# Two-layer attention trunk: layer B's first query block takes both key parts in one product, layer A's rotary key is turned before it is split, and a tenth warming product

## The chip, the core and the metric

The kernel runs on one core of a Trainium2 chip. The metric is device time in microseconds (us) from the first to the last instruction of one execution. The engines are TensorE (PE, with its weight loads shown apart as PEld), VectorE (DVE), ScalarE (ACT), GpSimd (POOL) and SyncE (SP), which issues most of the DMAs.

## What is computed

A decoder trunk of two layers over 512 tokens of width 1024, all in fp32. Layer A has multi-head latent attention (8 heads, a compressed key/value of rank 256, and one rotary key of 64 features that all heads share). Layer B has sliding-window attention: 16 query heads of 64 features over 4 shared key/value heads, in blocks of 128 queries, each of which sees its own block of keys and the one before; block 0 sees only its own. Each layer ends with a squared-ReLU MLP of width 4096, and every sum is normalised.

```python
# layer A: the scores' rotary part; k_r is one key for all heads
k_r = _rope(h[..., MLA_Q_RANK + MLA_KV_RANK:], pos)
s = (jnp.einsum('bqhc,bkc->bhqk', ql, c_kv)
     + jnp.einsum('bqhr,bkr->bhqk', qr, k_r)) * scale
...
# layer B
s = jnp.einsum('bnqkgd,bnjkd->bnkgqj', q, k_band) * SWA_HEAD_DIM ** -0.5
s = jnp.where(mask[None, :, None, None], s + bias, -jnp.inf)
m = jnp.maximum(s.max(-1), sink)
p = jnp.exp(s - m[..., None])
denom = p.sum(-1) + jnp.exp(sink - m)
o = jnp.einsum('bnkgqj,bnjkd->bnqkgd', p / denom[..., None], v_band)
```

## The kernel before, in words

**Numbers in two parts.** TensorE multiplies in a rounded fp32 form (F32R). To keep fp32 accuracy each operand is split: a high part, the rounded copy, written by ScalarE, and a low part, source minus high, written by VectorE (`split`, L75 to L83, where L77 is the copy and L80 the subtraction). A product of two such operands is three products into one bank (high by high, high by low, low by high). `group` (L102 to L106) issues the products of a bank; nearly all of TensorE's rows carry its line, L104. `pe` keeps an instruction at its place in program order on its engine; everything else may be moved by a scheduler when the program is built, which writes one fixed order for each engine. At run time each engine works through its own order, and waits on semaphores where an operand or a buffer is not ready.

**Start.** TensorE first multiplies a tile of zeros, WARM times, 512 columns each, into a bank that nobody reads (L342 to L345), while the first inputs come in. The first real products are layer A's compressed key/value: `kvb`, 320 columns for each block of 128 tokens, of which the last 64 are the rotary key.

**Layer A's rotary key** (`rot_key`, L944 to L951). For each block of tokens VectorE rotates the 64 features, writes them twice side by side, rounded, as the high part, and subtracts to get the low part; both go to `kr2`. Later, after the third block of the query latent, TensorE turns the high parts of the four blocks into one bank and the low parts into another (8 transposes, L1020), and ScalarE copies each bank to its half of `krr` (L1021). `krr` is read by layer A's scores (`scores`, L1106), from the first head on. For query block 0 layer A already takes the high and the low part of the keys in one product, 256 columns, and lets VectorE add the halves (L1125).

**Layer B's attention** (L1285 to L1383) runs over 16 heads with `run_steps`: at step u it issues the scores of head u + 2, then filling work (query products of later heads, at the end parts of the output projection), then the transposes of head u's probabilities (`turn`), then the product with the values of head u - 1 (`mix`).
- `scores`: for each of four query blocks, two products, with the keys' high part `khh` and low part `kll` (queries carry their low half in the other 64 rows). Blocks 1 to 3 have 256 keys; block 0 has 128. The four blocks fill two banks. VectorE adds the bias and takes the row maximum in one instruction for each block (L1320), then `nb` (L1324); ScalarE takes the exponentials to `p` (L1328) and that of the sink (L1332); VectorE adds and inverts the sums (L1333, L1334); GpSimd scales `p` (L1335, L1337). `p` has three buffers.
- `turn`: seven transposes (L1348, L1350), four into one "tr" bank and three into another; there are two such banks in the kernel. Each bank is emptied by a `split`: ScalarE writes `pth`, VectorE `ptl` (512 columns for the first bank, 384 for the second). The first bank's split is held behind the latest exponentials.
- `mix`: eight products; ScalarE copies the lower half of the rows (L1379), VectorE adds the halves (L1380).

After this the output projection, normalisations and the MLPs follow, the same for both layers; the change does not touch them.

Of the kernel before, what the change touches and what calls it, by code (L numbers as in the profile page):

```python
# [8 lines left out]
F32 = mybir.dt.float32  # L9
F32R = mybir.dt.float32r  # L10
AF = mybir.ActivationFunctionType
ALU = mybir.AluOpType
# [3 lines left out]
P = 128  # L16
D = 1024
S = 512
NT = S // P
# [6 lines left out]
SQH, SKVH, SHD = 16, 4, 64  # L26
# [5 lines left out]
LN_EPS, RMS_EPS = 1e-5, 1e-6  # L32
BANDW = 384
POOL_O, POOL_SO = (0, 2), (0, 1, 2)
WARM = 9

ON_POOL = ("w_h", "w_o", "w_sq", "w_so")

# [10 lines left out]
def build(tc, nc, io, out):  # L49
    with ExitStack() as top:  # L50
# [11 lines left out]
        def nm(s):  # L62
            n_names[0] += 1
            return f"{s}_{n_names[0]}"

        def bank(cols=512, tag="mm", bufs=6):
            return ps.tile([P, cols], F32, tag=tag, bufs=bufs, name=nm(tag), padded_shape=[P, 512])

        def tbank():
            return bank(512, "tr", 2)  # L70

        def f32(ap):
            return ap.bitcast(F32)

        def split(dst_h, dst_l, src, engine=None, keep=False):  # L75

            high = nc.scalar.activation(dst_h, src, AF.Copy)  # L77
            if keep:
                pe(high)
            low = (engine or nc.vector).tensor_sub(dst_l, src, f32(dst_h))  # L80
            if pinned[0] and engine is None:
                pe(low)
            return high, low  # L83

        def pe(ins):
            tc.keep_in_program_order(ins)
# [15 lines left out]
        def group(dst, pairs, first=True, last=True, **kw):  # L102
            for i, (st, mv) in enumerate(pairs):
                pe(nc.tensor.matmul(  # L104
                    dst, st, mv, start=first and i == 0, stop=last and i == len(pairs) - 1, **kw
                ))  # L106
# [237 lines left out]
        b = bank()  # L344
        group(b.rearrange("p (a b) -> p a b", a=4), [(zeros, zeros[:, None, :].broadcast_to([P, 4, P]))] * WARM)  # L345
        dummy = cp.tile([P, 1], F32, name="dummy")
# [32 lines left out]
        ident = cp.tile([P, P], F32, name="ident")  # L379
# [502 lines left out]
        with tc.tile_pool(name="mla", bufs=1) as mp:  # L882
# [11 lines left out]
            khh, kll = krr[:, 0, :], krr[:, 1, :]  # L894
# [34 lines left out]
            def rope(dst, src, t, n, other):  # L929

                s = src.rearrange("p (h d) -> p h d", h=n)
                d = dst.rearrange("p (h d) -> p h d", h=n)
                w = other.rearrange("p (h d) -> p h d", h=n)
                cb = cos[:, t : t + 1, :].broadcast_to([P, n, 64])
                nc.vector.tensor_mul(d, s, cb)
                for a, b in ((0, 32), (32, 0)):
                    sb = sin[:, t : t + 1, a : a + 32].broadcast_to([P, n, 32])
                    nc.vector.tensor_mul(w[:, :, a : a + 32], s[:, :, b : b + 32], sb)
                nc.vector.tensor_add(dst, dst, other)


            kr2 = mp.tile([P, 2, NT, P], F32, tag="kk", bufs=2, name=nm("kr2"))

            def rot_key(t, b):  # L944
                kr = sp.tile([P, 2, 64], F32, tag="kr", bufs=2, name=nm("kr"))
                rope(kr[:, 0, :], b[:, 256:320], t, 1, kr[:, 1, :])
                dup = kr[:, 0:1, :].broadcast_to([P, 2, 64])
                hh = kr2[:, 0, t, :].rearrange("p (a b) -> p a b", a=2)
                ll = kr2[:, 1, t, :].rearrange("p (a b) -> p a b", a=2)
                nc.vector.tensor_copy(hh.bitcast(F32R), dup)  # L950
                nc.vector.tensor_sub(ll, dup, hh)  # L951


            kvb = [bank(320) for _ in range(NT)]
# [30 lines left out]
            for t in range(NT):  # L985
                with tc.high_priority():
                    kvn.append(normed(kvb[t], KVR))
                rot_key(t, kvb[t])
# [6 lines left out]
            def query_latent(t, ks):  # L995
                tk = slice(t * P, (t + 1) * P)
                for k in ks:
                    wh, wl = ws[k // 2]
                    c = slice(k % 2 * QR, (k % 2 + 1) * QR)
                    group(qb[t], three(x0.h(k, tk), x0.l(k, tk), wh[:, c], wl[:, c]), k == 0, k == 7)  # L1000

            for t in range(NT):
                if t != 1:
                    qb[t] = bank(QR)
                if t == 0:
                    qb[1] = bank(QR)
                    for tt in range(2):
                        query_latent(tt, range(6))
                query_latent(t, range(6 if t < 2 else 0, KD))
                if t == 0:  # L1010
                    bias_bands()
                if t == 1:
                    with tc.high_priority():
                        normed_t(kvn, range(2), gkv, ckv)
                if t == 2:
                    with tc.high_priority():
                        for part, dst in ((0, khh), (1, kll)):
                            pt = tbank()
                            for tt in range(NT):
                                pe(nc.tensor.transpose(pt[:, tt * P : (tt + 1) * P], kr2[:, part, tt, :], ident))  # L1020
                            nc.scalar.activation(dst, pt, AF.Copy)  # L1021
                with tc.high_priority():
                    qn.append(normed(qb[t], QR))

# [173 lines left out]
            for t in range(2):  # L1198
                for kp in range(3):
# [3 lines left out]
            state["hold"] = hold  # L1203
            head_queries(1)
            run_steps([(h, i) for h in range(H) for i in range(NT)], AHEAD_S, scores, turn, mix, fill, NT, 2,
                      [lambda kp=kp: proj.part(2, kp) for kp in range(2)])

# [10 lines left out]
        mlp_pool[0] = None  # L1218

        with tc.tile_pool(name="swa", bufs=1) as mp:  # L1220
            khh = [mp.tile([P, S], F32R, name=nm("skh")) for _ in range(SKVH)]
            kll = [mp.tile([P, S], F32R, name=nm("skl")) for _ in range(SKVH)]

            def keys(m, cols, b):

# [41 lines left out]
            bias = [None] * 8  # L1267
# [29 lines left out]
            def scores(h, _):  # L1297
                j = h // GRP
                q = qs[h]
                nb = sp.tile([P, NT], F32, tag="nb", bufs=3, name=nm("nb"))  # L1300
                sm = sp.tile([P, NT], F32, tag="sm", bufs=3, name=nm("sm"))
                ri = sp.tile([P, NT], F32, tag="ri", bufs=3, name=nm("ri"))
                bs = []
                for n2 in range(2):
                    b = bank().rearrange("p (a b) -> p a b", a=2)
                    bs.append(b)
                    for a in range(2):
                        n = 2 * n2 + a
                        lo_c = P if n == 0 else 0
                        kc = slice(0, P) if n == 0 else slice((n - 1) * P, (n + 1) * P)  # L1310
                        tq = slice(n * P, (n + 1) * P)
                        group(b[:, a, lo_c:], [(q[:, tq], khh[j][:, kc]), (q[:, tq], kll[j][:, kc])])

                mx = bs[0][:, 0, 0:NT]
                for n2 in range(2):
                    for a in range(2):
                        n = 2 * n2 + a
                        lo_c = P if n == 0 else 0
                        b = bs[n2]
                        nc.vector.tensor_tensor_reduce(  # L1320
                            out=b[:, a, lo_c:], in0=b[:, a, lo_c:], in1=bias[h // 2][:, h % 2, lo_c:], op0=ALU.add,
                            op1=ALU.max, scale=1.0, scalar=NEG, accum_out=mx[:, n : n + 1],
                        )
                nc.vector.tensor_scalar(nb, mx, sink8[:, h : h + 1], -SWA_SCALE, ALU.max, ALU.mult)  # L1324
                p = mp.tile([P, NT, 256], F32, tag="p", bufs=3, name=nm("p"))
                for n in range(NT):
                    lo_c = P if n == 0 else 0
                    state["exp"] = nc.scalar.activation(  # L1328
                        p[:, n, lo_c:], bs[n // 2][:, n % 2, lo_c:], AF.Exp, bias=nb[:, n : n + 1],
                        scale=SWA_SCALE, accum_out=sm[:, n : n + 1],  # L1330
                    )
                nc.scalar.activation(ri, nb, AF.Exp, bias=sink[:, h : h + 1])  # L1332
                nc.vector.tensor_add(sm, sm, ri)  # L1333
                nc.vector.reciprocal(ri, sm)  # L1334
                nc.gpsimd.tensor_mul(p[:, 0, P:], p[:, 0, P:], ri[:, 0:1].broadcast_to([P, P]))  # L1335
                rest = ri[:, 1:].unsqueeze(2).broadcast_to([P, NT - 1, 256])
                nc.gpsimd.tensor_mul(p[:, 1:, :], p[:, 1:, :], rest)  # L1337
                ps_of[h] = p
# [180 lines left out]
```

## Time and profile before

| | us |
|---|---|
| median of 3 runs (range) | 997.25 (997.22 to 997.62) |
| span of the profiled execution | 997.4 |
| TensorE busy | 986.3 (99%) |
| VectorE busy | 771.9 (77%) |
| ScalarE busy | 554.7 (56%) |
| GpSimd busy | 216.5 (22%) |
| layer B's attention, 539 to 625: span, TensorE busy | 86.0, 84.27 |

How to read it: busy times are sums over the whole span, and the engines work side by side. A row of the timeline is start, duration, engine, line, operation, the tiles (written <- read), the shape and the count, and in brackets the idle time before it with what ended it. TensorE's products are pipelined and their ends modelled, so two neighbours' rows overlap; what one of them costs is read from start to start. Rows of groups give count, busy time and mean duration in ns. A wait's row gives the total, the number of times and the longest.

### The profile page before, as it was taken

How to read it: one execution, taken by the hardware profiler on the slowest of the kernel's cores; microseconds unless marked ns; L12 is line 12 of the kernel's file. 1: busy time of each engine (PE TensorE's matmuls, PEld its weight loads, DVE VectorE, ACT ScalarE, POOL GpSimd, SP SyncE). 2: the span in 40 equal slices, each digit the busy share in tenths (PEclk: the TensorE clock that was granted, in tenths of full speed). 3: DMA queues.
4: the chain of work that ended last, by engine and by line, in shares of the span. 5: the costliest groups of instructions: out<-in, count | busy, mean ns of one | idle time of the engine just before them, and what ended most of it. 6: DMA issues, size and time to landing. Idle time of an engine off the chain costs nothing.

```text
span 997.4 us, 15835 instructions
## 1 busy us (share of the span) xinstructions
PE 986.3 (99%) x6107; PEld 890.0 (89%) x6107; DVE 771.9 (77%) x1243; ACT 554.7 (56%) x850; POOL 216.5 (22%) x203
## 2 busy tenths in 40 slices
PE   9999999999999999999999999999999999999997
PEld 8988888998999999998898998889998999999986
DVE  5589967989778769877586778698985986898756
ACT  5457643467537637636145888546763664664620
POOL 0231101122212211210002775212131122123000
PEclk9999999999999999999999999999999999999999
DMA  7431126389879977963232212259798798798422
GB/s 249 143 89 54 64 106 224 92 174 243 157 171 241 175 174 202 230 118 125 87 106 96 85 65 75 96 158 208 195 187 187 166 214 175 162 263 147 117 93 85
DMA packets 60679, 149.55 MB, mean 150 GB/s; under 512 B 5260, under 2 KB 10301, under 8 KB 60605
## 3 DMA queue, kind: packets, MB, share of 16 engines
q0 software_dynamic: 24320, 58.73, 32.9%
q1 hardware_dynamic: 36140, 89.56, 27.1%
q8 instruction: 48, 0.79, 0.3%
q10 hardware_dynamic: 144, 0.26, 0.1%
q14 instruction: 27, 0.21, 0.1%
HBM read 146.41 MB, written 4.22 MB: 151 GB/s over the span
## 4 chain that ended last, share of the span: by engine, by line
PE 96%; DVE 2%; ACT 1%; DMA 1%; issue 0%; POOL 0%; DVEq 0%; SPq 0%; ACTq 0%
PE mm L104 88%; PE tr L104 5%; PE tr L1159 1%; PE tr L663 1%; PE tr L1348 1%; ACT wh L77 1%; PE tr L1350 0%; DMA raw<-in_w_kv 0%; PE tr L437 0%; DMA raw<-in_w_h 0%; DVE mm L1320 0%; DVE ptl L80 0%; PE tr L924 0%; DVE ql L80 0%; POOL wl L80 0%
## 5 line engine op out<-in xcount | busy, mean ns | idle before, releaser
L104 PE MATMUL mm<-wh,fac 128*128 128x512 f32 (+1 forms) x944 | 292.8, 387 | 0.0
L77 ACT ACTIVATE wh<-wq 128x1024 fp32r<-128x1024 f32 x164 | 173.6, 1060 | 183.6 <-PE mm L104 131.4
L80 DVE TENSOR_TENSOR wl<-wq,wh 128x1024 fp32r<-128x1024 f32 x164 | 199.7, 1222 | 70.9 <-ACT wh L77 70.1
L104 PE MATMUL mm<-xth,wh 128*128 128x256 f32 (+1 forms) x928 | 243.7, 291 | 0.0
L104 PE MATMUL mm<-xth,wl 128*128 128x256 f32 (+1 forms) x800 | 233.5, 292 | 0.0
L104 PEld LDWEIGHTS mm<-wh,fac 128*128 128x128 f32 x944 | 176.3, 188 | 35.4 <-DVE fac L80 0.6
L104 PE MATMUL mm<-xtl,wh 128*128 128x256 f32 (+1 forms) x672 | 197.4, 294 | 0.0
L104 PE MATMUL mm<-wl,fac 128*128 128x512 f32 (+1 forms) x472 | 182.4, 387 | 0.0
L104 PEld LDWEIGHTS mm<-xth,wh 128*128 128x128 f32 x928 | 168.9, 192 | 3.1
L104 PEld LDWEIGHTS mm<-xth,wl 128*128 128x128 f32 x800 | 153.4, 192 | 2.6
L77 ACT ACTIVATE wh<-raw 128x1024 fp32r<-128x1024 f32 (+3 forms) x86 | 85.0, 989 | 95.1 <-PE mm L104 56.4
L199 POOL DMA_DIRECT2D wq<-in_up x64 | 77.5, 1228 | 257.7 <-DVE wl L80 189.0
L104 PEld LDWEIGHTS mm<-xtl,wh 128*128 128x128 f32 x672 | 128.9, 192 | 3.0
L80 DVE TENSOR_TENSOR wl<-raw,wh 128x1024 fp32r<-128x1024 f32 (+2 forms) x66 | 77.1, 1174 | 35.1 <-ACT wh L77 34.7
L104 PEld LDWEIGHTS mm<-wl,fac 128*128 128x128 f32 x472 | 88.9, 188 | 16.6
L199 POOL DMA_DIRECT2D wq<-in_down x48 | 42.0, 875 | 187.5 <-DVE wl L80 181.6
L80 POOL TENSOR_TENSOR wl<-raw,wh 128x1024 fp32r<-128x1024 f32 (+2 forms) x20 | 41.2, 2063 | 87.6 <-ACT wh L77 81.9
L104 PE MATMUL mm<-wh,oh 128*128 128x512 f32 x128 | 50.9, 398 | 0.0
L104 PE MATMUL mm<-wh,ol 128*128 128x512 f32 x128 | 50.2, 392 | 0.0
L104 PE MATMUL mm<-wl,oh 128*128 128x512 f32 x128 | 50.0, 390 | 0.0
L398 POOL TENSOR_TENSOR rs<-mv,half 128x1 f32<-128x1 f32 x16 | 11.0, 689 | 167.2 <-DVE mv L419 167.1
L563 DVE TENSOR_TENSOR x<-mm,x 128x512 f32<-128x512 f32 (+1 forms) x49 | 32.9, 676 | 14.5 <-PE mm L104 14.5
(217 smaller groups left out, 1822.3 us busy)
## 6 DMA issues: line engine op xcount, KB each, us to landing
wq<-in_up POOLq DMA_DIRECT2D x64, 512.0 KB, 8.5
wq<-in_down POOLq DMA_DIRECT2D x48, 512.0 KB, 7.1
wq<-in_up SPq DMA_DIRECT2D x32, 512.0 KB, 7.0
raw<-in_down SPq DMA_DIRECT2D x28, 512.0 KB, 6.8
wq<-in_down SPq DMA_DIRECT2D x24, 512.0 KB, 5.4
raw<-in_up SPq DMA_DIRECT2D x16, 512.0 KB, 4.6
raw<-in_w_o SPq DMA_DIRECT2D x8, 512.0 KB, 4.2
raw<-in_w_sq SPq DMA_DIRECT2D x8, 512.0 KB, 3.3
```

What stands on the lines that cost most here:

```text
L77: high = nc.scalar.activation(dst_h, src, AF.Copy)
L80: low = (engine or nc.vector).tensor_sub(dst_l, src, f32(dst_h))
L104: pe(nc.tensor.matmul(dst, st, mv, start=first and i == 0, stop=last and i == len(pairs) - 1, **kw))
L199: nc.gpsimd.dma_start(half(a, jp), chunk(*more, jp), accum_op=ALU.add)
L398: nc.gpsimd.tensor_tensor(r, v, half, ALU.pow)
L563: nc.vector.tensor_add(xs[t][:, c], b, xs[t][:, c])
L663: pe(nc.tensor.transpose(pt[:, a, :], xs[t][:, k * P : (k + 1) * P], ident))
L1159: pe(nc.tensor.transpose(pt[:, kb * P : (kb + 1) * P], p[:, kb * P : (kb + 1) * P], ident))
L1348: pe(nc.tensor.transpose(pt[:, a, 0:P], p[:, kb, P:256], ident))
```

## The change

Three edits. (1) In layer B the keys' two parts lie side by side in one tile `kk`, and block 0's two products of 128 columns become one of 256, over two runs of 128; VectorE adds the first half of the result to the bias into `p`, and the maximum of block 0 takes that sum in place of the bias. `p` is therefore claimed before the maxima and no longer after them. The products of the other blocks stay. (2) In layer A the rotary key is written once, in fp32, turned with four transposes into one bank, and split from there: high part by ScalarE, low part by VectorE. (3) WARM goes from 9 to 10. The scheduler's order on TensorE and SyncE differs by nothing else; on VectorE, ScalarE and GpSimd it also differs within layer B's attention.

```diff
-WARM = 9
+WARM = 10
...
-            kr2 = mp.tile([P, 2, NT, P], F32, tag="kk", bufs=2, name=nm("kr2"))
+            kr2 = mp.tile([P, NT, P], F32, tag="kk", bufs=2, name=nm("kr2"))
...
                 dup = kr[:, 0:1, :].broadcast_to([P, 2, 64])
-                hh = kr2[:, 0, t, :].rearrange("p (a b) -> p a b", a=2)
-                ll = kr2[:, 1, t, :].rearrange("p (a b) -> p a b", a=2)
-                nc.vector.tensor_copy(hh.bitcast(F32R), dup)
-                nc.vector.tensor_sub(ll, dup, hh)
+                nc.vector.tensor_copy(kr2[:, t, :].rearrange("p (a b) -> p a b", a=2), dup)
...
-                        for part, dst in ((0, khh), (1, kll)):
-                            pt = tbank()
-                            for tt in range(NT):
-                                pe(nc.tensor.transpose(pt[:, tt * P : (tt + 1) * P], kr2[:, part, tt, :], ident))
-                            nc.scalar.activation(dst, pt, AF.Copy)
+                        pt = tbank()
+                        for tt in range(NT):
+                            pe(nc.tensor.transpose(pt[:, tt * P : (tt + 1) * P], kr2[:, tt, :], ident))
+                        split(khh, kll, pt)
...
-            khh = [mp.tile([P, S], F32R, name=nm("skh")) for _ in range(SKVH)]
-            kll = [mp.tile([P, S], F32R, name=nm("skl")) for _ in range(SKVH)]
+            kk = [mp.tile([P, 2, S], F32R, name=nm("skk")) for _ in range(SKVH)]
+            khh, kll = [[k[:, part, :] for k in kk] for part in range(2)]
...
-                        group(b[:, a, lo_c:], [(q[:, tq], khh[j][:, kc]), (q[:, tq], kll[j][:, kc])])
-
+                        if n == 0:
+                            both = b[:, 0, :].rearrange("p (a b) -> p a b", a=2)
+                            group(both, [(q[:, tq], kk[j][:, :, kc])])
+                        else:
+                            group(b[:, a, :], [(q[:, tq], khh[j][:, kc]), (q[:, tq], kll[j][:, kc])])
+
+                p = mp.tile([P, NT, 256], F32, tag="p", bufs=3, name=nm("p"))
+                first = p[:, 0, 0:P]
+                nc.vector.tensor_add(first, bs[0][:, 0, 0:P], bias[h // 2][:, h % 2, P:])
...
-                            out=b[:, a, lo_c:], in0=b[:, a, lo_c:], in1=bias[h // 2][:, h % 2, lo_c:], op0=ALU.add,
+                            out=b[:, a, lo_c:], in0=b[:, a, lo_c:],
+                            in1=first if n == 0 else bias[h // 2][:, h % 2, :], op0=ALU.add,
                             op1=ALU.max, scale=1.0, scalar=NEG, accum_out=mx[:, n : n + 1],
...
-                p = mp.tile([P, NT, 256], F32, tag="p", bufs=3, name=nm("p"))
```

## The prediction, made before the changed kernel ran

> **What bounds the kernel now.** I read the page first (busy shares and the chain that ended last), then the groups of instructions by form on TensorE, then the timeline of the three places that the change touches, then the waits inside layer B's attention.
>
> ```profile
> span 997.4 us, 15835 instructions
> PE 986.3 (99%) x6107; PEld 890.0 (89%) x6107; DVE 771.9 (77%) x1243; ACT 554.7 (56%) x850; POOL 216.5 (22%) x203
> ...
> PE 96%; DVE 2%; ACT 1%; DMA 1%; issue 0%; POOL 0%; DVEq 0%; SPq 0%; ACTq 0%
> ```
>
> TensorE (PE) is busy for 99% of the span and makes 96% of the chain. So the price of a product is the time until the next one starts, and whatever it frees comes off the end, unless PE then waits elsewhere. PE waits little, and in layer B's attention only for VectorE (DVE); the stage's row follows the wait's (PE 84.27, PEld 75.71, DVE 64.59, ACT 71.53, POOL 54.01 of 86 us).
>
> ```profile
> PE tr L1348 <- DVE ptl L80: 1.7, 3, 0.9
> ```
>
> ```profile
> 539.00:625.00 86.00, 84.27 (x554) 75.71 (x553) 64.59 (x230) 71.53 (x214) 54.01 (x44) 1.00 0.24 80
> ```
>
> **Layer B: 32 short products become 16.** The timeline of one head's eight score products (head 13, the other heads look alike):
>
> ```profile
> 608.12 0.27 PE L104 MATMUL mm<-skh,q 128*128 128x128 f32 x1
> 608.23 0.27 PE L104 MATMUL mm<-skl,q 128*128 128x128 f32 x1
> 608.35 0.33 PE L104 MATMUL mm<-skh,q 128*128 128x256 f32 x1
> 608.51 0.28 PE L104 MATMUL mm<-skl,q 128*128 128x256 f32 x1
> 608.63 0.28 PE L104 MATMUL mm<-skh,q 128*128 128x256 f32 x1
> ...
> 609.11 0.40 PE L104 MATMUL mm<-wh,oh 128*128 128x512 f32 x1
> ```
>
> Eight products take 609.11 - 608.12 = 0.99 us. From start to start a 256-wide product takes 0.12 (608.51 to 608.63); the two 128-wide ones take 608.35 - 608.12 = 0.23 together, so each costs as much as a 256-wide one. Seven products should take 0.88: the first 256-wide one keeps its 0.16. That is 0.11 a head. For heads 0 to 2, whose scores follow 512-wide products, I reckon 0.09 (estimate: the first short product is partly hidden there). Sum: 13 x 0.105 + 3 x 0.09 = 1.6 us. That the moving operand is now two runs of 128 costs nothing: layer A already reads krr so, at 286 ns mean, where head 13's unbroken 256-wide products last 0.28.
>
> ```profile
> L104 PE MATMUL mm<-krr,qr 128*128 128x256 f32 x24 | 5.6, 286 | 0.0
> ```
>
> [...] Head 13's rows say 0.23 against 0.12 us; the measurement decides.
>
> Added are 16 tensor_adds on DVE. Layer A has the same one (L1125, 128x128 out of a bank), 284 ns:
>
> ```profile
> L1125 DVE TENSOR_TENSOR p<-mm,const x8: 274/284/293, 64.2 to 131.5; 128x128 f32<-128x128 f32 x8
> ```
>
> That is 16 x 0.29 = 4.6 us. DVE idles 86 - 64.6 = 21 us in the stage, so its total hides the adds. They do lengthen a chain: scores, the maxima (L1320), nb, exponentials, the copies out of the transposes' two "tr" banks (pth on ScalarE, then ptl on DVE), and the next head's transposes, which need those banks. The add waits for PE's products, which the maximum waited for already; p has three buffers, and the transposes that free the oldest precede these products on PE, so its earlier claim costs nothing. If that cover were gone, each add would cost 0.3.
>
> Where that chain is late is the end of the stage, heads 10 to 12. DVE first, then PE:
>
> ```profile
> 608.79 0.68 DVE L1292 TENSOR_TENSOR q<-mm,q 64x512 fp32r<-64x512 f32 x1
> 609.40 0.28 DVE L1320 CUSTOM_DVE_ANT_0 mm<-mm,bias 128x128 f32<-128x128 f32 x1
> ...
> 609.72 0.43 DVE L1320 CUSTOM_DVE_ANT_0 mm<-mm,bias 128x256 f32<-128x256 f32 x1
> ...
> 610.74 0.66 DVE L80 TENSOR_TENSOR ptl<-tr,pth 128x512 fp32r<-128x512 f32 x1
> ...
> 616.51 0.66 DVE L80 TENSOR_TENSOR ptl<-tr,pth 128x512 fp32r<-128x512 f32 x1
> 617.10 0.68 DVE L1380 TENSOR_TENSOR o<-mm,low 64x512 f32<-64x512 f32 x1
> ```
>
> ```profile
> 611.55 0.30 PE L1348 MATMUL tr<-ident,p 128*128 128x128 f32 x1 [0.89 <-DVE ptl L80]
> ...
> 617.23 0.33 PE L1348 MATMUL tr<-ident,p 128*128 128x128 f32 x1 [0.66 <-DVE ptl L80]
> ```
>
> These are the first and the last of the three waits, each for a ptl. DVE works in program order, and the changed program's order differs here by more than the two adds, so I rework it on before's clock. After q ends at 609.40 DVE issues ptl384 of head 10, the add and the first two maxima of head 13, sm, recip, then ptl512 of head 10. By the rows' spacings: 609.40 + 0.55 (ptl384) + 0.3 (add) + 0.32 and 0.45 (maxima) + 0.2 (sm, recip) + 0.59 (ptl512, as 616.51 to 617.10) = 611.8. Until the next ptl512 (head 11) come two maxima, q and two o (0.61 each, as 608.79 to 609.40), ptl384, the second add, head 14's four maxima and four tiny ones: 0.9 + 1.8 + 0.55 + 0.3 + 1.7 + 0.5 + 0.59 = 6.3, so it ends at 618.1. Before it ended at 617.1. Head 12's second half of transposes therefore starts about 1.0 later than at 617.23; PE needs 0.1 less from there to head 13, so the tail gives back about 0.9 us. That is the largest uncertain term. Its ends: a gain of 0.8 (half of the 1.7 of waits goes) and a loss of 2 (they more than double). I take the 0.9, since the reckoning follows DVE's known order.
>
> Earlier, at heads 3 to 10, the same bank is the tight spot. Head 7's rows, DVE first, then the start of PE's next transposes:
>
> ```profile
> 589.20 0.66 DVE L80 TENSOR_TENSOR ptl<-tr,pth 128x512 fp32r<-128x512 f32 x1
> 589.77 0.21 DVE L1324 TENSOR_SCALAR nb<-mm,sink 128x4 f32<-128x4 f32 x1
> 589.90 0.55 DVE L80 TENSOR_TENSOR ptl<-tr,pth 128x384 fp32r<-128x384 f32 x1
> ```
>
> ```profile
> 590.31 0.27 PE L1348 MATMUL tr<-ident,p 128*128 128x128 f32 x1
> ```
>
> The first bank is free at 589.77, the second at 590.45, and the transposes want them at 590.31 and, four of 0.11 later, 590.75: 0.54 and 0.30 of cover. The add takes 0.3 and PE's earlier arrival 0.1, which leaves from 0.1 to -0.1. In all I count 0.2 for these heads.
>
> Layer B: -1.6 + 0.9 + 0.2 = -0.5.
>
> **Layer A: the rotary key.** Eight transposes become four, one ScalarE copy goes, four DVE subtractions of 0.29 go, and one of a 512-wide bank comes.
>
> ```profile
> L1020 PE MATMUL tr<-ident,kr x8: 272/272/273, 35.9 to 36.7; 128*128 128x128 f32 x8
> L951 DVE TENSOR_TENSOR kr<-kr,kr x4: 281/292/292, 24.7 to 28.4; 128x128 f32<-128x128 f32 x4
> ```
>
> ```profile
> L104 PE MATMUL mm<-krr,qr x56: 278/337/398, 63.5 to 139.7; 128*128 128x256 f32 x24, 128*128 128x384 f32 x16, 128*128 128x512 f32 x16
> ```
>
> Starts run from 35.9 to 36.7 for eight: 0.11 apart, so 4 x 0.11 = 0.44 us off PE, which never waits there. The low half now follows the high one by a DVE pass over 512 columns (0.66, as ptl), near 38; its first reader is at 63.5, which hides it 25 us deep. Without that cover it would cost 0.7. The key is written by 28.4 and turned at 35.9, so the four subtractions were hidden and are worth nothing.
>
> **The tenth warming product.**
>
> ```profile
> 1.00 4.21 PE L104 MATMUL mm<-zeros 128*128 128x512 f32 x9 [1.00 <-POOL zeros L343]
> 5.74 1.44 PE L104 MATMUL mm<-wh,xth 128*128 128x320 f32 x4 [0.53 <-ACT wh L77]
> 8.03 1.27 PE L104 MATMUL mm<-wl,xth 128*128 128x320 f32 x4
> 9.10 0.92 PE L104 MATMUL mm<-wh,xth 128*128 128x320 f32 x4
> 9.86 0.74 PE L104 MATMUL mm<-wh,xtl 128*128 128x320 f32 x4
> 10.44 0.75 PE L104 MATMUL mm<-wl,xth 128*128 128x320 f32 x4
> ```
>
> The nine end at 5.21; the first real product then waits 0.53 for its weights. A tenth costs about 0.43 (4.21 less the first one's latency, over nine) and ends near 5.64, before 5.74: it is hidden by that wait. If the weights came 0.5 earlier it would cost its 0.43. Its worth is the other question. Four 320-wide products take 9.10 - 8.03 = 1.07 us until about 9.4 and 10.44 - 9.86 = 0.58 after: TensorE runs at nearly half rate for 3.7 us of real work, in spite of 4.2 us of warming. A gap of 0.53 lies between the two. If closing it brought the full rate forward to the first real products, the 3.7 us hold 3.7 / 0.267 = 14 of them, each 0.12 cheaper (1.07 - 0.58 over four): 1.7 us saved. The ends are 0 and 1.7; I take 0, because nine products and 4.2 us did not do it, and a gap of 0.1 remains.
>
> [...]
>
> **Sum.** Forecast: -0.44 (A) - 0.5 (B) + 0 (warming) = -0.94 on the profiled 997.4. The median of the runs is 997.25, 0.15 below; so 996.3.
>
> **Rivals.**
> 1. [...] Chance 0.38.
> 2. The tail gives nothing back, and layer B keeps its 1.6: -2.0, 995.2. For it: PE waits only 1.7 in all now. Against: DVE's order above. 0.08.
> 3. On the other side: DVE's longer chain holds up PE at every head, not only at the last. Place: ptl before the transposes, heads 3 to 10. Price: the 0.3 of the add at each of the eight heads, up to +2.4, in all +1.5, 998.7. It decides from 0.12 a head (0.94 / 8) on. For it: head 7's cover, which the add uses up. Against: DVE has 21 us idle in the stage. 0.08.
> 4. The change does not save what it says: with the short products no dearer than half a long one, B loses the 0.9 and 0.2 and gains nothing: -0.44 + 1.1 = +0.7, 997.9. Head 13's rows speak against it. 0.04.
>
> **How the numbers follow.** The forecast has 0.42; its own range is 995.3 to 997.4. A measurement of this kernel can tell about 0.2%, 2.0 us, from no change. Faster by more than that: 0.7 of rival 1 (its -2.5 lies just beyond, within about 0.9 either way), half of rival 2 and a little of the forecast, 0.33. Slower by over 2.0: the far part of rival 3, 0.04. The rest, 0.63, is within. The range for 8 in 10 reaches from rival 1 with a milder tail, 994.0, to the near part of rival 3, 998.0; about 0.1 is left out below it and 0.07 above.
>
> **What would show it.** 112 score products in place of 128, seven in 0.88 us a head; four transposes near 36; the zeros x10, and the first real product still at 5.74. [...] For the tail: a transpose of head 12 that starts about 1.0 late against head 10's, waiting for ptl, and no other long wait before it. It is wrong if PE's waits in layer B come to under 1 us or over 4, or if the 256-wide first product takes over 0.2.

## The result

The changed kernel takes **999.93 us** (median of 20 runs, 998.63 to 1001.97); the kernel before, on the same chips, 997.74 (20 runs, 996.74 to 999.91). The ratio is 1.002, 95% interval 1.0013 to 1.0026: 2.2 us slower, and outside the range of the forecast (994.0 to 998.0).

The device time of a run is its span and about 1.75 us (1.72 to 1.95 in all runs): the profiled execution after has a span of 998.1 and a time of 999.86. So the profiled execution before, span 997.4, would by that have a time of some 999.1 (an estimate, as its own time is not on record) and not 997.25: at its start TensorE took 1.06 to 1.23 us for a group of four products until about 9.4, where the profiles of e1_warm, e2_key and the changed kernel show 0.58 or 0.59 from 6.4 on at the latest (below).

The page of the changed kernel (span; busy times; the chain by engine):

```profile
span 998.1 us, 15800 instructions
...
PE 984.5 (99%) x6088; PEld 886.3 (89%) x6088; DVE 777.7 (78%) x1256; ACT 555.0 (56%) x849; POOL 216.4 (22%) x203
...
PE 91%; DVE 3%; ACT 2%; DMA 2%; issue 1%; POOL 0%; SPq 0%; DVEq 0%; ACTq 0%
```

TensorE is busy 1.8 us less, but before's slow start (about 1.7 us) is in that difference, so it is not the work saved. Its share of the chain fell from 96 to 91%: VectorE, ScalarE and DMA are longer links of it. TensorE's waits over the whole span (total, times, longest), then layer B's stage, 539 to 625:

```profile
PE tr L1351 <- DVE ptl L80: 2.8, 3, 2.0
...
PE mm L104 <- ACT p L1331: 0.7, 3, 0.4
PE tr L437 <- DVE xtl L80: 0.5, 1, 0.5
PE tr L663 <- DVE x L425: 0.5, 1, 0.5
```

```profile
539.00:625.00 86.00, 82.67 (x530) 73.23 (x529) 69.52 (x244) 70.32 (x212) 54.00 (x44) 1.00 0.22 75
```

VectorE's busy time in the stage rose from 64.59 to 69.52, the added sums, and TensorE's fell from 84.27 to 82.67: the work left it, and the time became idle time. The waits for `ptl` rose from 1.7 to 2.8; three waits for `p` are new. Where they stand, in TensorE's timeline (the bracket is the idle time before the row and what ended it):

```profile
564.43 0.50 PE L104 MATMUL mm<-xth,wh 128*128 128x512 f32 x1 [0.41 <-ACT p L1331]
...
586.15 0.50 PE L104 MATMUL mm<-xth,wh 128*128 128x512 f32 x1 [0.17 <-ACT p L1331]
...
607.88 0.50 PE L104 MATMUL mm<-wh,oh 128*128 128x512 f32 x1 [0.17 <-ACT p L1331]
...
610.58 0.33 PE L1351 MATMUL tr<-ident,p 128*128 128x128 f32 x1 [0.58 <-DVE ptl L80]
...
616.94 0.33 PE L1351 MATMUL tr<-ident,p 128*128 128x128 f32 x1 [2.00 <-DVE ptl L80]
...
618.21 1.04 PE L104 MATMUL mm<-skk,q 128*128 128x256 f32 x7
619.09 0.40 PE L104 MATMUL mm<-wh,oh 128*128 128x512 f32 x1
```

The last two rows show the saving as forecast: seven score products in 619.09 - 618.21 = 0.88 us, where eight took 0.99. But behind the scores of heads 5, 9 and 13 the filling products wait for a bank that ScalarE's exponentials, those of heads 4, 8 and 12, have not finished reading, and head 12's second half of transposes waits 2.00 us, where it waited 0.66. The start and layer A:

```profile
1.00 4.53 PE L104 MATMUL mm<-zeros 128*128 128x512 f32 x10 [1.00 <-POOL zeros L343]
5.63 0.86 PE L104 MATMUL mm<-wh,xth 128*128 128x320 f32 x4
6.33 0.75 PE L104 MATMUL mm<-wh,xtl 128*128 128x320 f32 x4
...
34.16 0.60 PE L1016 MATMUL tr<-ident,kr 128*128 128x128 f32 x4
34.52 0.42 PE L104 MATMUL mm<-wh,xth 128*128 128x384 f32 x1
```

Here groups of four already start 0.58 apart from about 6 on (6.33 to 6.91 in the next row), which is the upper end of the prediction's warming term (1.7 us), and four transposes stand in layer A in place of eight. The profile's own clock does not tell the two starts apart: from 5.74 to 9.50 it gives a granted clock of 1.00 (third figure from the end) in both kernels, where TensorE issues 14 products before and 26 after. Before's row:

```profile
5.74:9.50 3.76, 3.76 (x14) 3.76 (x15) 3.47 (x7) 2.80 (x6) 0.00 (x0) 1.00 1.03 363
```

So that the clock was what held up before's start is inferred from the rate (1.07 us in place of 0.58 for a group of four); no figure shows it.

### The profile page after: what moved, and what is told of

The parts are those of the page before. It is cut to its first block, busy times and chain, and to the rows that moved or that the text cites. A ratio compares the mean times of both kernels' runs of the same rounds, so it can differ in the third digit from the quotient of the medians.

```text
span 998.1 us, 15800 instructions
## 1 busy us (share of the span) xinstructions
PE 984.5 (99%) x6088; PEld 886.3 (89%) x6088; DVE 777.7 (78%) x1256; ACT 555.0 (56%) x849; POOL 216.4 (22%) x203
## 4 chain that ended last, share of the span: by engine, by line
PE 91%; DVE 3%; ACT 2%; DMA 2%; issue 1%; POOL 0%; SPq 0%; DVEq 0%; ACTq 0%
PE mm L104 84%; PE tr L104 5%; ACT wh L77 1%; PE tr L1155 1%; PE tr L663 1%; DMA wq<-in_up 1%; DMA raw<-in_w_v 1%; PE tr L1351 1%; ACT p L1331 1%; DMA raw<-in_w_kv 0%; DVE x L425 0%; DVE wl L80 0%; PE tr L1353 0%; DMA raw<-in_w_h 0%; DVE mm L1323 0%
```

## The experiments

**Theory 1.** The added sum lengthens the chain from the scores to the exponentials; what TensorE saves turns into waits, above all at head 12. **Theory 2**, the rival, differs from run to run: the scheduler's new order, the sum as mere VectorE time, or a chain in which TensorE's pause is a symptom only. Each kernel was timed beside the kernel before (997.2 to 997.6 each time), 11 runs of each (5 of e3_swa, e9_late and e11_late_key_free); ratios are against it. One more term came up on the way: the granted clock.

### The three edits one by one

e1_warm has only `WARM = 10`, e2_key only the edit of the rotary key, e3_swa only layer B's. e4_swa_add is e3_swa with the merged product taken apart again, so that only the sum is added:

```diff
-                            both = b[:, 0, :].rearrange("p (a b) -> p a b", a=2)
-                            group(both, [(q[:, tq], kk[j][:, :, kc])])
+                            for part in range(2):
+                                group(b[:, 0, part * P : (part + 1) * P], [(q[:, tq], kk[j][:, part, kc])])
```

> Only the tenth warming product. In the profile of the changed kernel the products ran at the full rate from the first real one (start 5.63 against 5.74, shift -1.7 us by 9.5). If the clock's rise is the gap's doing, this alone gains up to 1.7 us in a run whose clock rose late, about 1 us in the median, and nothing elsewhere: -1.0. Rival (the rise falls by chance, whatever the tenth product): 0 within 0.3.

> Only layer A's key turned in fp32. Four transposes of 0.11: -0.44 us at 36 us, and if TensorE stays the bound, at the end too. Rival (an earlier TensorE only waits for later DMAs, as the changed kernel did at 518 and 656): 0.

> Only layer B's edit. Theory 1 (the added VectorE step and the order that comes with it delay the exponentials and the tr banks): slower, +2 to +3.5 us in all, with TensorE waits of 4 to 6 us in layer B's attention. Theory 2 (layer B loses little and the rest is DMA chance outside it): -0.5 to +0.5.

> Layer B's edit with the two short products kept apart (high part to the first half of the bank, low part to the second, then the same VectorE addition): the addition without the saved product. Theory 1: 1.6 us above the kernel with the product merged, +3.5 to +5 against before. Theory 2: TensorE hides the addition, +0 to +0.5.

| | median us (range) | ratio, 95% |
|---|---|---|
| e1_warm | 997.71 (997.17 to 998.91) | 1.0005 (0.9996 to 1.0014) |
| e2_key | 997.86 (996.74 to 999.31) | 1.0005 (0.9996 to 1.0014) |
| e3_swa | 1000.78 (1000.60 to 1001.07) | 1.0035 (1.0023 to 1.0048) |
| e4_swa_add | 999.28 (997.83 to 999.57) | 1.0013 (1.0005 to 1.0022) |

Warming and key are worth nothing that can be measured; all of the loss is layer B's edit, and there the sum alone costs less than the sum with the saving, which theory 1 did not say. That the early full rate does not need the tenth product is seen in e2_key's record, which has nine and a longer gap behind them (1.02 us) than before:

```profile
1.00 3.64 PE L104 MATMUL mm<-zeros 128*128 128x512 f32 x9 [1.00 <-POOL zeros L343]
5.67 0.86 PE L104 MATMUL mm<-wh,xth 128*128 128x320 f32 x4 [1.02 <-ACT wh L77]
6.36 0.74 PE L104 MATMUL mm<-wh,xtl 128*128 128x320 f32 x4
6.94 0.75 PE L104 MATMUL mm<-wl,xth 128*128 128x320 f32 x4
```

Groups of four are 0.58 apart from the second one on, so the rise at 9.4 in the profile of before was that execution's. What made e3_swa dearer than e4_swa_add is in its windows (busy of PE, PEld, DVE, ACT, POOL; granted clock; DMA) and in its TensorE rows:

```profile
609.00:618.00 9.00, 6.37 (x43) 5.26 (x43) 7.70 (x30) 7.44 (x24) 4.56 (x5) 1.00 0.14 54
618.00:622.00 4.00, 4.00 (x18) 3.63 (x18) 2.65 (x9) 1.93 (x7) 2.22 (x3) 0.57 0.02 4
622.00:627.00 5.00, 5.00 (x31) 4.35 (x30) 1.96 (x8) 2.76 (x11) 1.29 (x1) 1.00 0.00 2
```

```profile
617.09 0.33 PE L1355 MATMUL tr<-ident,p 128*128 128x128 f32 x1 [2.02 <-DVE ptl L80]
...
618.61 1.80 PE L104 MATMUL mm<-skk,q 128*128 128x256 f32 x7
620.21 0.63 PE L104 MATMUL mm<-wh,oh 128*128 128x512 f32 x1
620.63 0.63 PE L104 MATMUL mm<-wl,oh 128*128 128x512 f32 x1
...
621.48 0.39 PE L104 MATMUL mm<-wh,oh 128*128 128x512 f32 x1
```

Head 12's pause is 2.02 us, and behind it the granted clock is 0.57 over 618 to 622: seven score products take 620.21 - 618.61 = 1.60 in place of 0.88, for about 3.4 us (618.0 to 621.4). The fall follows that pause, with another of 0.60 at 610.7 before it; in the profile of the whole change, pauses of 2.00 (616.94) and 0.58 (610.58) left the clock at 1.00.

### Is the clock part of the price? The pause filled

Six products of zeros, 1.4 us, between the halves of head 12's transposes, into the bank that the next product claims anyway; e5_fill on e3_swa (the other engines' orders stay the same), e10_after_fill on the whole change, e15_add_fill on e4_swa_add, e16_before_fill on the kernel before:

```diff
+FILL = 6
...
+                    if h == 12 and k2 == 1:
+                        early[0] = bank()
+                        group(
+                            early[0].rearrange("p (a b) -> p a b", a=4),
+                            [(zeros, zeros[:, None, :].broadcast_to([P, 4, P]))] * FILL,
+                        )
                     pt = tbank().rearrange("p (a b) -> p a b", a=2)
...
-                b = bank()
+                b = early[0] if h == 11 else bank()
```

> Layer B's edit alone, and six products of zeros (128x512, 0.23 us each, 1.4 us) put between the two halves of head 12's transposes, where TensorE stood still for 2.0 us; the orders of VectorE, ScalarE and GpSimd are those of e3_swa. Theory 1: the pause itself costs what the four engines' chain makes of it, and on top of it the granted clock falls to half for 3.4 us after it (e3_swa's record shows 0.57 over 618 to 622), 1.7 us more; with the pause filled the clock stays at 1.00 and the time falls from 1000.8 to 998.9 to 999.4. Theory 2: the chain from scores to exponentials alone sets the end, and the clock's fall is made up behind it: 1000.6 to 1001.1, unchanged.

> The whole change, with six products of zeros (1.4 us) in head 12's pause, as in e5_fill. Theory 1: the change's own time, 999.9, has executions with and without the fall of the clock after head 12 (998.6 to 1002.0); filled, those above 1000 go and the median is 998.3 to 999.0. Theory 2: the spread has another source and the fill only delays: 999.8 to 1000.5.

> e4_swa_add (two products kept apart, VectorE's sum added: 999.28, 997.8 to 999.6) with six products of zeros in head 12's pause, which was 1.4 us there. Theory 1: the pause was near what costs the clock, so its slower executions lost it; filled, 997.8 to 998.5. Rival: its 1.8 us are the chain alone and the products of zeros, as long as the pause, add nothing or a little: 999.2 to 999.7.

> The kernel before with six products of zeros (1.4 us) in head 12's pause of 1.7 us. Theory 1: most executions of the kernel before keep their clock there, so the median stays at 997.1 to 997.5, and the few above 998.5 (5 or 6 in 27) go. Rival: the clock has no part in before's spread: the same median and the same few above 998.5.

| | unfilled | filled (range) | ratio of the filled, 95% |
|---|---|---|---|
| e5_fill | 1000.78 | 998.74 (997.94 to 999.71) | 1.0016 (1.0007 to 1.0025) |
| e10_after_fill | 999.93 | 998.36 (997.36 to 998.79) | 1.0006 (0.9997 to 1.0015) |
| e15_add_fill | 999.28 | 998.62 (998.08 to 1000.54) | 1.0017 (1.0008 to 1.0025) |
| e16_before_fill | 997.43 | 997.71 (997.32 to 1000.44) | 1.0008 (0.9999 to 1.0017) |

More work made two kernels faster: by 2.0 us where the fall is on record, and by 1.6 on the whole change, of whose 20 unfilled runs 17 lie above the slowest filled one (998.79). e5_fill's record, windows and TensorE:

```profile
609.00:618.00 9.00, 7.94 (x53) 6.87 (x54) 7.02 (x27) 7.48 (x25) 5.21 (x6) 1.00 0.02 7
618.00:622.00 4.00, 4.00 (x26) 3.46 (x25) 3.47 (x13) 1.25 (x3) 2.75 (x3) 1.00 0.00 0
```

```profile
613.55 1.64 PE L105 MATMUL mm<-zeros 128*128 128x512 f32 x6
615.81 0.33 PE L1363 MATMUL tr<-ident,p 128*128 128x128 f32 x1 [0.61 <-DVE ptl L81]
...
617.09 1.05 PE L105 MATMUL mm<-skk,q 128*128 128x256 f32 x7
617.97 0.40 PE L105 MATMUL mm<-wh,oh 128*128 128x512 f32 x1
```

TensorE still waits for `ptl`, so the fill took nothing from the chain; but it is busy, and the clock stays at 1.00. For the whole change the clock is argued from this: the fill's gain is measured (the ratios fall from 1.0020 to 1.0006), but in the one record of the unfilled change the clock stays at 1.00 behind the pause, and yet its time, 999.86, is the median. That execution loses time elsewhere: TensorE waits 0.49 us at 517 and 0.47 at 656, each behind a weight transfer of 6 us, which neither e3_swa nor e10_after_fill shows there. From head 15's scores to the end it takes 379.9 us, e10_after_fill 378.8, and e3_swa, with the fall, 380.4. On the kernel before there is nothing to win, and the two late runs there (above 1000) stay. The expectations speak of a pause of 1.7 at its head 12; that is the sum of three waits (0.89, 0.18 and 0.66), of which the last alone stands where the fill goes. With the sum alone (e15_add_fill) the medians differ by 0.7 and the ratios hardly, which leaves it open whether that kernel loses its clock.

### What does the sum cost without the clock?

e6_merge keeps the merged product and leaves out the sum. The two parts change places in `kk`, so that the maximum reads the high part's scores, and the low part of the first block's keys is missing from the scores:

```diff
-            khh, kll = [[k[:, part, :] for k in kk] for part in range(2)]
+            kll, khh = [[k[:, part, :] for k in kk] for part in range(2)]
...
-                first = p[:, 0, 0:P]
-                nc.vector.tensor_add(first, bs[0][:, 0, 0:P], bias[h // 2][:, h % 2, P:])
...
-                            in1=first if n == 0 else bias[h // 2][:, h % 2, :], op0=ALU.add,
+                            in1=bias[h // 2][:, h % 2, lo_c:], op0=ALU.add,
```

> The merged product alone: the first block's low-part scores are computed in the same product but not added (VectorE's added sum is left out, so the low part of the first block's keys is missing from the scores). TensorE's saved 0.1 us a head is there, VectorE's chain is that of before. Theory 1: TensorE comes 1.6 us sooner to a bank that comes free no sooner, so the pause at head 12 grows from 1.7 to about 3 us, nothing is gained (997.0 to 997.6), and in those executions in which the clock then falls to half 1.7 us are lost (up to 999.2). Theory 2, the added sum is the whole cost and the saved products count in full: 995.8 to 996.3.

Measured: 996.44 (995.68 to 999.07), ratio 0.9995 (0.9986 to 1.0004), 0.8 below before by the medians, though the interval does not exclude no gain, and below theory 1's range: head 12's pause does not grow (0.70, before 0.66). That VectorE's and ScalarE's work starts with the scores and moves up with them would explain it. TensorE's rows of the first score products of heads 3 and 10 and of head 12's second half, first of e6_merge, then of the changed kernel:

```profile
552.54 0.36 PE L104 MATMUL mm<-skk,q 128*128 128x256 f32 x1
...
589.73 0.45 PE L104 MATMUL mm<-skk,q 128*128 128x256 f32 x2
...
614.75 0.33 PE L1353 MATMUL tr<-ident,p 128*128 128x128 f32 x1 [0.70 <-DVE ptl L80]
```

```profile
552.37 0.48 PE L104 MATMUL mm<-skk,q 128*128 128x256 f32 x2
...
590.68 0.45 PE L104 MATMUL mm<-skk,q 128*128 128x256 f32 x2
```

Head 10's in the kernel before, for comparison:

```profile
591.96 0.27 PE L104 MATMUL mm<-skh,q 128*128 128x128 f32 x1
```

Heads 3 to 10 take 37.19 us without the sum and 38.31 with it, 1.1 more; from there to head 12's second half (616.94 in the changed kernel) 25.02 and 26.26, 1.2 more. Together 2.4; and e5_fill against e6_merge, timed side by side, says 998.74 - 996.44 = 2.3.

That is the price of the sum together with the order that the scheduler made for it, and at heads 3 to 10 the order takes part. There the scores of most heads follow each other after 5.28 to 5.42 us, but from head 5 to 6 it is 5.98 and from head 9 to 10 5.73, where e6_merge takes 5.34 and 5.33. That is 0.64 and 0.40 more, nearly the whole 1.1, from recorded waits of 0.41 and 0.17. Just ahead of the exponentials that these waits end with (those of heads 4 and 8) ScalarE's order has a copy to `pth`, which takes 0.37. First the changed kernel at head 4, then e4_swa_add at head 8:

```profile
562.62 0.59 ACT L1287 ACTIVATE q<-mm 64x512 fp32r<-64x512 f32 x1
563.11 0.47 ACT L77 ACTIVATE pth<-tr 128x384 fp32r<-128x384 f32 x1
563.48 0.35 ACT L1331 ACTIVATE p<-mm,nb 128x128 f32<-128x128 f32 x1
```

```profile
585.12 0.59 ACT L1291 ACTIVATE q<-mm 64x512 fp32r<-64x512 f32 x1
585.62 0.35 ACT L1335 ACTIVATE p<-mm,nb 128x128 f32<-128x128 f32 x1
```

In the kernel before and in e6_merge the exponentials of heads 4, 8 and 12 follow `q` directly, and no such wait is there. e4_swa_add has the sum in the same place and, of these three heads, the copy ahead at head 4 alone; it waits once, 0.31 behind head 5's scores. So the sum without the copy ahead made no wait there, in a kernel whose TensorE is 0.1 a head slower; no run keeps the sum and the saved products and changes this order alone, which leaves the shares of sum and order open.

### Can the wait be taken away?

e7_free (on e3_swa) and e8_base_free (on before) let head 11's first split, whose `ptl` head 12's transposes wait for, go before the exponentials of head 13:

```diff
-                        with behind((state["exp"],)):
+                        with behind(None if h in (11,) else (state["exp"],)):
```

e12_key_free is e8_base_free with layer A's key as in the change. e17_key_so3 has the key and moves the 1.23 us split of a weight chunk, which stands ahead of head 12's maxima on VectorE, to GpSimd (`POOL_SO = (0, 1, 2, 3)`); e18_key_free_so3 has both.

> Layer B's edit alone, with head 11's first split (four transposes, 512 wide) no longer held in turn behind the exponentials of head 13. Theory 1: head 12's second half of transposes waits for this split to free its bank; released, the wait falls from 2.0 us to under 0.7, the clock stays at 1.00, and the time falls from 1000.8 to 997.3 to 998.5. Theory 2: the chain through maxima and exponentials sets the end and the split of 0.6 us on ScalarE and 0.7 on VectorE now stands ahead of it: 1000.6 to 1001.5.

> The kernel before, with head 11's first split no longer held in turn behind the exponentials of head 13; nothing else changed. Theory 1: the 1.7 us for which TensorE waits at head 12 shrink by about 1 us, and the executions that lose the clock there go: 996.0 to 996.9, against 997.4. Theory 2: no gain, or 0.3 to 0.6 later, as the split stands ahead of the exponentials: 997.4 to 998.0.

> Layer A's rotary key as in the change and head 11's first split not held, layer B's products as before. Theory 1: e8_base_free's 997.1 less up to 0.4: 996.6 to 997.1. Rival: the key's 0.4 us is taken up again by waits behind layer A, as in e2_key: 997.1 to 997.5.

> Layer A's key as in the change, layer B's products as before, and the split of the fourth output-weight chunk (1.23 us on VectorE at 607.5, ahead of head 12's maxima) moved to GpSimd (2.4 us there). Theory 1 (VectorE's chain sets the wait of 1.7 us at head 12): 0.5 to 1.2 below the kernel before, 996.1 to 996.9. Rival (GpSimd's 2.4 us stand in the way of its products with the reciprocals, or the chain through ScalarE's exponentials is as late): 997.0 to 998.0.

> e17_key_so3 with head 11's first split not held in turn behind head 13's exponentials. Theory 1: the two take the same wait away, so no more than 0.3 below the better of e12_key_free (997.0) and e17_key_so3: 996.0 to 996.8. Rival: as e12_key_free, 996.9 to 997.5.

| | median us (range) | ratio, 95% |
|---|---|---|
| e7_free | 998.01 (997.23 to 1000.64) | 1.0010 (1.0001 to 1.0019) |
| e8_base_free | 997.08 (995.97 to 998.45) | 0.9996 (0.9987 to 1.0005) |
| e12_key_free | 997.03 (996.23 to 998.17) | 0.9997 (0.9988 to 1.0005) |
| e17_key_so3 | 997.62 (996.91 to 998.23) | 0.9997 (0.9988 to 1.0006) |
| e18_key_free_so3 | 997.98 (996.88 to 999.69) | 1.0004 (0.9995 to 1.0014) |

e7_free gains 2.8 us on e3_swa, as theory 1 expected, but its waits in layer B's stage say that most of it is not the wait:

```profile
PE mm L104 <- ACT p L1335: 2.4, 4, 1.2
PE tr L1355 <- DVE ptl L80: 0.6, 1, 0.6
```

The wait for `ptl` fell from 2.6 to 0.6, and that for the exponentials rose from 0.6 to 2.4: one long pause became several shorter ones, of 3.0 us in all against 3.2, and the clock stayed at 1.00. On the kernel before, whose record shows the clock at 1.00 there, the same edit gains nothing certain. e17_key_so3 is a miss for theory 1, by the same exchange (its waits over the whole span):

```profile
PE tr L1344 <- DVE nb L1320: 0.9, 1, 0.9
...
PE mm L104 <- ACT p L1324: 0.7, 1, 0.7
```

No wait for `ptl` is left, and 1.6 us of others stand there, where before had 1.7. No version was found that is measurably faster than the kernel before and computes the same.

### Is it the sum's place or its length?

e9_late takes block 0's maximum over the high part alone and adds the low part behind the last maximum; the first block's exponential goes last. For that the four maxima needed a place of their own:

```diff
-                nc.vector.tensor_add(first, bs[0][:, 0, 0:P], bias[h // 2][:, h % 2, P:])
-                mx = bs[0][:, 0, 0:NT]
+                mx = sp.tile([P, NT], F32, tag="mx", bufs=3, name=nm("mx"))
...
-                            out=b[:, a, lo_c:], in0=b[:, a, lo_c:],
-                            in1=first if n == 0 else bias[h // 2][:, h % 2, :], op0=ALU.add,
+                            out=p[:, 0, P:] if n == 0 else b[:, a, lo_c:], in0=b[:, a, lo_c:],
+                            in1=bias[h // 2][:, h % 2, lo_c:], op0=ALU.add,
...
+                nc.vector.tensor_add(p[:, 0, P:], p[:, 0, P:], bs[0][:, 0, 0:P])
+                for n in (1, 2, 3, 0):
```

e13_late_psum puts the maxima back into the bank (`mx = bs[0][:, 0, P : P + NT]`). e11_late_key_free and e14_late_psum_key_free are these two with layer A's key and head 11's split freed.

> Layer B's edit, with the added sum taken off the way to the maxima: the first block's maximum is taken over the high part's scores alone, and VectorE adds the low part after the last maximum, while the exponentials of blocks 1 to 3 run; the first block's exponential is the last one. VectorE's work is as long as in e3_swa, the same products are saved. Theory 1 (the sum costs as a link of the chain from scores to exponentials, 0.3 us a head, and the pause it makes then costs the clock): most of the 4.3 us between e3_swa and e6_merge comes back, 996.4 to 997.6. Theory 2 (it costs as VectorE time, wherever it stands, with VectorE at 83 per cent and splits queued behind it): 999.0 to 1001.

> e9_late with layer A's rotary key turned in fp32 as in the change, and head 11's first split not held behind head 13's exponentials. Theory 1: the saved products (0.8 us by e6_merge), the key's 0.4 us and some of e8_base_free's 0.2: 995.8 to 997.0, below the kernel before. Theory 2 (sum costs wherever it stands): 997.0 to 998.5, as e7_free.

> e9_late with the four maxima of a head kept in PSUM, in the first block's scores that are read by then, in place of an SBUF tile; all else as e9_late. There the scaling of the maxima (128x4) took 0.90 us in the mean, and it ended with GpSimd's instruction each time. Theory 1 (the sum costs as a link ahead of the exponentials): with the scaling back at 0.22 us the time is 996.4 to 998.0. Theory 2 (the sum costs wherever it stands on VectorE): 999.5 to 1001. If the scaling is as dear as before, the place of the maxima is not what made it dear: 1003 to 1004.

> e13_late_psum with layer A's rotary key turned in fp32 and head 11's first split not held. Theory 1: 0.2 to 0.4 below e13_late_psum, 996.0 to 997.2, and so below the kernel before. Theory 2: 997.5 to 998.5, as e7_free.

| | median us (range) | ratio, 95% |
|---|---|---|
| e9_late | 1003.81 (1001.87 to 1004.64) | 1.0061 (1.0048 to 1.0074) |
| e11_late_key_free | 1003.45 (1001.98 to 1004.85) | 1.0058 (1.0044 to 1.0072) |
| e13_late_psum | 998.29 (997.72 to 999.73) | 1.0010 (1.0001 to 1.0019) |
| e14_late_psum_key_free | 999.37 (998.04 to 1001.53) | 1.0020 (1.0011 to 1.0029) |

The first two are misses for every theory, and e13_late_psum shows that the place of the maxima was the cause, worth 5.5 us together with the clock that it cost (the last section has the rows). With that mended, the late sum stands between the two theories' ranges: 2.5 below e3_swa, 0.45 below e5_fill, and 1.9 above e6_merge. The profiled executions give the place a larger share: from head 3's scores to head 15's e6_merge takes 63.48 us, e13_late_psum 64.70 and e5_fill 65.59. So part of the sum's price remains wherever it stands; how much its place explains, from 0.45 of 2.3 to 0.9 of 2.1, stays open, and e13_late_psum's order on ScalarE is another as well (no copy ahead of the exponentials of heads 4, 8 and 12). e14_late_psum_key_free is slower than e13_late_psum by 1.1 in the medians, against every expectation, though the intervals overlap; its profiled execution was its fastest run (span 996.3) and shows no cause. That stays open.

## Why the prediction was wrong, point by point

- **Layer B's saving: right per head, wrong at the end.** 112 products, seven in 0.88 us, as forecast. Of the 1.6 us, 0.8 reach the end by e6_merge's median; by its interval (0.9986 to 1.0004) not the whole 1.6. Per product before's rows give 0.115 us for a 128-wide one (0.23 for two) and 0.12 for a 256-wide one.
- **Layer B's chain: the step that failed, and in it the term "In all I count 0.2 for these heads".** The forecast gave back 0.9 in the tail and 0.2 at heads 3 to 10, together 1.1. Measured against e6_merge the sum and its order cost 2.3: 1.2 in the tail and 1.1 at heads 3 to 10. The tail was right: from head 10's scores to head 12's second half 26.26 us pass where before took 617.23 - 591.96 = 25.27, so it starts 1.0 late, waiting for `ptl`, as foreseen. At heads 3 to 10 the prediction checked only the two "tr" banks, and only with VectorE's rows of before. The waits are for a product bank: the exponentials of heads 4 and 8 end later, behind the added sum and a copy that ScalarE's new order puts ahead of them, and the filling products want their bank. The text "no other long wait before it" was wrong by these (0.41 and 0.17, and 0.17 at head 13). The third rival had the sign, but its place was another (`ptl` before the transposes), its price there was up to 2.4, and it was given 0.08.
- **The clock after the pause: not foreseen.** In e3_swa's record a pause of 2.02 us costs more than its length: the granted clock behind it is 0.57 over 618 to 622. The fill takes 1.6 us off the whole change, whose own record shows no fall. The forecast asked about the clock only at the start.
- **Layer A's key: mechanism right, gain not found.** Four transposes in place of eight are there; e2_key does not show 0.44 us at the end. Later waits could absorb an early TensorE: in e2_key's record it waits 0.7 for `x` (L663), and in the changed kernel's 0.5, where before's had no such row. But e1_warm and e13_late_psum, which do not have the key's edit, wait 0.4 and 0.7 there too. So where the 0.44 went is not shown, and an effect of that size lies within the interval.
- **The tenth warming product: the 0 was right by luck, and the rival at 0.38 was wrong.** The reason given for the 0 was that nine products do not raise the clock in time. In the profiles of e1_warm, e2_key and the changed kernel groups of four stand 0.58 or 0.59 apart from the second group on, with nine products or ten (the first group takes 0.76, 0.69 and 0.70 us, in e3_swa and e6_merge 1.24). No run shows the gain that the rival's -2.5 and the range's lower end, 994.0, rest on: e1_warm, whose ten products leave no gap, and e2_key, with a gap of 1.02 us, start alike, and neither's time differs from before's by what can be measured. One execution with a late rise was read as the kernel's habit.
- **The base.** A span was set beside a median of device times, which are 1.75 longer; the likeness of 997.4 and 997.25 was chance. With that, the slow start of the profiled execution would have been noticed: by that difference it was 1.9 above the median.
- **The sum again, with what was measured:** -0.8 (products) + 2.3 (added sum and order) + 1.6 (what filling the pause takes off) + 0 (warming, key) = +3.1, against +2.2 measured. The rest is within what the intervals leave; how many executions of the change lose the clock was not seen, as the mean clocks of the single runs (0.996 to 0.999) do not sort them.

## What to carry to other kernels

Before an instruction is added to a side engine, follow its chain to every buffer that it frees, product banks as well as transpose banks, and through the new order of every engine on that chain: an engine with idle time in its total (here VectorE, busy 69.52 of 86.0 us in the stage) can still be late at each of them. Price a new pause of TensorE with what the clock may lose behind it (in e3_swa 0.57 over 4 us, behind 2.02 us of pause), and where a pause can't be removed, filling it with idle products can be worth more than it costs (six of them, 1.4 us, took 2.0 us off e3_swa and 1.6 off the whole change). Compare a profiled execution with the distribution of the runs in one and the same metric before building a sum on it.

## What the runs showed of the hardware that was not expected

**With the maxima in SBUF a small instruction took four times as long, and its long rows ended with GpSimd's.** In e9_late the scaling of a head's four maxima (`nb`, 128x4) takes 904 ns in the mean, in e13_late_psum, where it reads the bank, 220. VectorE's group of each kernel, then two of e9_late's instructions with the GpSimd rows at the same time:

```profile
L1330 DVE TENSOR_SCALAR nb<-mx,sink 128x4 f32<-128x4 f32 x15 | 13.6, 904 | 0.2
```

```profile
L1330 DVE TENSOR_SCALAR nb<-mm,sink 128x4 f32<-128x4 f32 x16 | 3.5, 220 | 0.3
```

```profile
557.73 1.76 DVE L1330 TENSOR_SCALAR nb<-mx,sink 128x4 f32<-128x4 f32 x1
...
613.24 1.53 DVE L1330 TENSOR_SCALAR nb<-mx,sink 128x4 f32<-128x4 f32 x1
```

```profile
554.71 4.76 POOL L80 TENSOR_TENSOR wl<-raw,wh 128x1024 fp32r<-128x1024 f32 x2
...
613.27 1.47 POOL L1343 TENSOR_TENSOR p<-p,ri 128x768 f32<-128x768 f32 x1
```

Each ends 0.02 or 0.03 us after GpSimd's instruction does (559.49 and 559.47; 614.77 and 614.74), however short its own work; so do the rows at 565.23 and 607.98, by 0.04 and 0.03 (566.60 and 566.56; 609.15 and 609.12), while the one at 601.15 takes 0.23. In the second pair VectorE's row starts 0.03 us ahead of GpSimd's and is long all the same. That it waits for GpSimd is the author's reading of the common ends; by what it would be held up no row shows. Moving the maxima's tile from the bank to SBUF cost 5.5 us on the whole kernel; the fall of the clock is in that figure, as in e9_late's record the granted clock is 0.55 from 614 to 618 us and 0.60 from 618 to 622, and in e13_late_psum's it stays at 1.00.

**The clock fell inside the kernel, after 2.02 us without products,** to 0.57 over 618 to 622 in e3_swa's record, where products were slow for 3.4 us; in e5_fill's, with six products of zeros in the pause, it stayed at 1.00. In the changed kernel's record a pause of 2.00 us left it at 1.00, and in e9_late's, with 0.55 from 614 to 618, the pauses are 1.83 us (to 613.47) and 1.27 (to 615.37), so the length of the pause alone does not decide.
